# Where a streaming encoder layer splits its weights: the order of the up stage, of the weight sums, and of the last residual row

## The chip, the cores and the metric

The kernel runs on one core of one Trainium2 chip. Its time is device time in microseconds (us), the median of the runs of one kernel. A core has five engines with queues of their own, which run beside each other and wait for one another by semaphores: TensorE (PE in the profile; PEld are its weight loads), VectorE (DVE), ScalarE (ACT), GpSimd (POOL) and SyncE (SP), which here only starts DMA transfers.

## The reference, cut to what matters

One layer of an encoder over 1152 tokens (1024 of a prompt, 8 x 16 of decoding samples), all in float32:

```python
h  = rms_norm(x, g_norm_mix);  z = h @ w_in            # split into latents, keys, gates ga, gb ...
x  = x + (sigmoid(ga) * (A @ w_oa) + sigmoid(gb) * (R @ w_or)) @ w_out
u  = rms_norm(x, g_norm_ffn) @ w_ffn_up                # 1024 -> 2 x 2816, gate and value halves
c  = up[:, 0:T]*cw[0] + up[:, 1:T+1]*cw[1] + up[:, 2:T+2]*cw[2] + bias   # causal conv, width 3
x  = x + (silu(c_gate) * c_val) @ w_ffn_down
```

`A` is latent attention, `R` retention; both, and the states that are returned, are outside the change.

## The kernel before

**Precision.** Each float32 factor is split into two parts: ACT casts the high part (`whi`, `xt`, `act` ..., line 228), DVE subtracts it from the source (line 229, `wlo` and its like). A product is then three matmuls, high by high, high by low and low by high. So each weight piece that is loaded costs a cast on ACT and a subtraction on DVE before PE can use it.

**Stages around the change.** (1) The gate stage makes tiles of the gate projection; the kv stage follows later. (2) The mix stage runs three layers of eight output tiles each, `w_or`, `w_oa` and `w_out`, through `layer` (line 1243); a tile is 72 matmuls into three PSUM tiles of 384 columns, and its result is evicted by DVE (lines 1275, 1282 and, in w_out, 1294). w_out's eviction adds the residual row from `x`, and its rows go in the order 0, 4, 1, 5, 2, 6, 3, 7. (3) The up stage has 22 `Pair`s, each one gate and one value tile of 128 channels over all tokens. (4) The down stage makes 24 tiles of 66 matmuls, of which the first two are computed together.

**The pair.** The up projection of a pair is done with seven products (`products`, line 1353; n = 0 to 6) of 24 matmuls of 128 x 288 instead of eight, by Winograd's scheme: the rows are combined into seven blocks (b11, t2, b21, t3, t1, t4, b22, each in four parts over k; line 1324 and 1327 are two of the subtractions), and the weights into sums. The products accumulate in three banks: p (n = 0, 2), q (n = 1, 3, 5) and r (n = 4, 6). After some of the products `then(n, ..)` reads a bank that the next product in it goes on adding to: `read_u2` after n = 1 and `read_u3` after n = 3 (both line 1404), c11 after n = 2 (L1420), c21 and c12 at the end. Around these reads DVE and ACT do the rest of the work for the pair before: the three conv taps of value (`cv`) and gate (`cg`, taps at L1451 and L1455), Silu (L1538), the product of both (L1459, L1462), a store of the result to `s_act`, and for the pair after, the splits of its four weight pieces w[0] to w[3] (`prep(i)`; w[3] is 512 wide, the others 1024).

**Weight sums.** Three of the four pieces of a pair come from sums of weight quarters. POOL makes them (`sums`, L344 to L347) from loads of `w_up` (`prg`, `prv`, `pr`) and stores them in DRAM (`s_w`): eleven full sets in the gate stage, then the others in halves, one half after each tile of the mix stage (`presum_half`). The raw buffers of the halves are those of w[3] and its high part (tags w3, h3).

**Row blocks.** Blocks that have a place in memory during w_out are split there; the others go to DRAM (`s_t`, `s_b`) and come back as `z` (two buffers; `reload`), each with its two splits.

**What sets the order.** A scheduler orders the instructions by its own estimate, except inside `in_order(engines)`, which keeps the named engines' instructions as they are written. FOUR is PE, ACT, DVE and POOL. Before, a pair is in FOUR order, but for pair 0, where PE alone is fixed; the down stage's two first tiles are not in a fixed order. DMA queues on SP and POOL run in order.

## Time and profile before

| | us |
|---|---|
| median of 3 runs (least, most) | 2517.89 (2517.13, 2523.43) |
| profiled execution | 2519.17 |
| its span, first to last instruction | 2517.2 |
| PE, DVE, ACT, POOL busy | 2405.0, 1415.6, 938.6, 453.8 |
| mean granted clock | 0.98 |
| w_out ends, pair 0 begins | 1675.78 |
| pair 1 begins | 1716.92 |
| sixth product of pair 1, of pair 21 | 1733.31, 2224.81 |

A timeline row gives start, duration, engine, line, operation, output and inputs with their shapes, how many instructions are grouped, and in brackets the idle time before and what ended it. A row of waits gives the engine and line that waited, what for, the total, the number of times and the longest. In a chain (start, duration, what) each piece was released by the one before.

### The profile page before, as it was taken

The numbers are of one execution on the slowest core, as the hardware profiler recorded it, in microseconds if no ns is written. First come the engines' busy times: TensorE is split into PE (matmuls) and PEld (weight loads), VectorE is DVE, ScalarE is ACT, GpSimd is POOL, SyncE is SP. The second block draws the span as 40 slices with busy tenths as digits, with TensorE's granted clock in tenths as the row PEclk, the third lists the DMA queues.
The fourth block names the chain that finished last, engine by engine and source line by source line (L and its number), as shares of the span: only waits on it lengthen the run. The fifth ranks groups of instructions, "written<-read, shape, count | busy, mean of one in ns | idle before, by whom it ended". The sixth has DMA issues, their size and how long they took to land.

```text
span 2517.2 us, 38532 instructions
## 1 busy us (share of the span) xinstructions
PE 2405.0 (96%) x14888; PEld 2290.5 (91%) x14888; DVE 1415.6 (56%) x2857; ACT 938.6 (37%) x2210; POOL 453.8 (18%) x734
## 2 busy tenths in 40 slices
PE   8999999999999999999999989979999999999999
PEld 8999998898999978888999989968999999989999
DVE  6233456546259766446884235367777777775442
ACT  5121332333246555664663112243333333243331
POOL 4701001001013212331111432321000000111100
PEclk9999999999999999998999999989999999999999
DMA  7932220111125676228766555562232323367752
GB/s 266 372 127 106 94 69 23 61 63 41 64 89 177 207 241 208 95 80 220 197 170 199 190 182 176 179 213 93 92 104 91 108 94 105 103 199 240 228 165 90
DMA packets 176935, 366.29 MB, mean 146 GB/s; under 512 B 15344, under 2 KB 93296, under 8 KB 175088
## 3 DMA queue, kind: packets, MB, share of 16 engines
q1 hardware_dynamic: 82528, 213.00, 25.9%
q0 software_dynamic: 35968, 88.52, 11.4%
q10 hardware_dynamic: 58256, 62.30, 7.3%
q8 instruction: 117, 1.92, 0.3%
q14 instruction: 66, 0.54, 0.1%
HBM read 252.65 MB, written 111.13 MB: 145 GB/s over the span
## 4 chain that ended last, share of the span: by engine, by line
PE 71%; DMA 9%; DVE 9%; POOL 4%; issue 3%; ACT 3%; SPq 1%; ACTq 0%; POOLq 0%; DVEq 0%
PE mm L188 43%; PE mm L1365 16%; DMA pr<-w_up 4%; PE sm L188 4%; PE sc L188 3%; DVE wlo L229 2%; PE apo L188 2%; ACT whi L228 1%; PE apt L1126 1%; DVE cv L1459 1%; POOL psum L347 1%; POOL psum L345 1%; POOL psum L344 1%; DVE rl L229 1%; POOL psum L346 1%
## 5 line engine op out<-in xcount | busy, mean ns | idle before, releaser
L229 DVE TENSOR_TENSOR wlo<-wraw,whi 128x1024 fp32r<-128x1024 f32 (+3 forms) x223 | 260.8, 1176 | 301.2 <-ACT whi L228 300.1
L228 ACT CAST whi<-wraw 128x1024 fp32r<-128x1024 f32 (+3 forms) x223 | 217.8, 992 | 388.7 <-PE mm L188 319.6
L1365 PE MATMUL mm<-xt,whi 128*128 128x288 f32 x1408 | 291.0, 301 | 43.3 <-DVE u L1404 34.2
L1365 PEld LDWEIGHTS mm<-xt,whi 128*128 128x128 f32 x1408 | 230.8, 192 | 48.8 <-DVE u L1404 39.1
L188 PE MATMUL mm<-whi,xh 128*128 128x256 f32 (+2 forms) x720 | 228.2, 333 | 0.7 <-DVE gsig L398 0.7
L188 PE MATMUL mm<-whi,xl 128*128 128x256 f32 (+2 forms) x720 | 225.3, 329 | 0.0
L188 PE MATMUL mm<-wlo,xh 128*128 128x256 f32 (+2 forms) x720 | 224.8, 329 | 0.3 <-DVE wlo L229 0.3
L1365 PE MATMUL mm<-xb,whi 128*128 128x288 f32 x1056 | 212.2, 295 | 0.0
L1365 PE MATMUL mm<-xt,wlo 128*128 128x288 f32 x704 | 211.1, 300 | 0.0
L1365 PEld LDWEIGHTS mm<-xb,whi 128*128 128x128 f32 x1056 | 170.3, 189 | 0.3
L188 PE MATMUL mm<-rh,whi 128*128 128x384 f32 x576 | 136.8, 344 | 25.7 <-DVE mg L1294 9.1
L1365 PE MATMUL mm<-xb,wlo 128*128 128x288 f32 x528 | 156.0, 295 | 0.0
L188 PEld LDWEIGHTS mm<-whi,xl 128*128 128x128 f32 x720 | 132.5, 190 | 12.1
L188 PEld LDWEIGHTS mm<-whi,xh 128*128 128x128 f32 x720 | 132.6, 190 | 10.6 <-issue 0.7
L188 PE MATMUL mm<-act,whi 128*128 128x384 f32 x528 | 136.4, 337 | 5.8 <-ACT act L228 3.4
L188 PEld LDWEIGHTS mm<-wlo,xh 128*128 128x128 f32 x720 | 132.6, 190 | 9.8 <-DVE wlo L229 0.5
L188 PE MATMUL mm<-rl,whi 128*128 128x384 f32 x576 | 134.8, 341 | 3.6 <-DVE rl L229 3.6
L188 PE MATMUL mm<-act,dwhi 128*128 128x384 f32 x528 | 135.4, 335 | 0.0
L1365 PEld LDWEIGHTS mm<-xt,wlo 128*128 128x128 f32 x704 | 135.4, 192 | 0.0
L188 PE MATMUL mm<-rh,wlo 128*128 128x384 f32 x576 | 133.8, 340 | 0.0
L188 PEld LDWEIGHTS mm<-rh,whi 128*128 128x128 f32 x576 | 105.7, 193 | 28.5 <-ACT whi L228 9.3
L188 PE MATMUL mm<-xh,whi 128*128 128x384 f32 x528 | 123.8, 340 | 3.9 <-ACT whi L228 3.1
(492 smaller groups left out, 5679.3 us busy)
## 6 DMA issues: line engine op xcount, KB each, us to landing
wraw<-w_dn SPq DMA_DIRECT2D x48, 512.0 KB, 3.6
s_q<-uqT ACTq DMA_DIRECT2D x36, 384.0 KB, 3.1
aq<-s_q POOLq DMA_DIRECT2D x8, 1536.0 KB, 9.9
ar<-s_act POOLq DMA_DIRECT2D x21, 576.0 KB, 6.1
s_w<-psum POOLq DMA_DIRECT2D x11, 1024.0 KB, 9.6
pr<-w_up SPq DMA_DIRECT2D x44, 256.0 KB, 4.7
s_w<-psum POOLq DMA_DIRECT2D x22, 512.0 KB, 4.5
wraw<-w_up SPq DMA_DIRECT2D x22, 512.0 KB, 3.8
```

Source lines behind the costliest of these rows:

```text
L188: E.matmul(out, l, r, start=start, stop=stop)
L228: A.copy(hi, src)
L229: return V.tensor_tensor(out=lo, in0=src, in1=hi.bitcast(F32), op=ALU.subtract)
L344: G.tensor_tensor(out=s[:, 1], in0=rg[:, 0], in1=rv[:, 0], op=ALU.add)
L345: G.tensor_tensor(out=s[:, 2], in0=rv[:, 0], in1=rv[:, 1], op=ALU.add)
L346: G.tensor_tensor(out=s[:, 0], in0=s[:, 2], in1=rg[:, 0], op=ALU.add)
L347: G.tensor_tensor(out=s[:, 3], in0=s[:, 0], in1=rg[:, 1], op=ALU.add)
L1126: E.transpose(pt[:, j * 256 + e * P:j * 256 + (e + 1) * P], pm[e][:, jj * P:(jj + 1) * P], ident)
L1365: E.matmul(banks[bank][c], l[:, ks], x, start=bool(first) and k + e == 0, stop=k + e == 5, skip_group_check=not first)
L1459: V.tensor_tensor(out=cv[:, :SEQ], in0=cg[:, :SEQ], in1=cv[:, :SEQ], op=ALU.mult)
```

## The change

Up stage: within a pair the taps come first, the split of w[3] moves from the end of the pair before to n = 1 of its own pair, and the product moves ahead of `prep(0)`; the order is fixed for pair 0 too. DVE in a steady pair, from the 512 wide `wlo` (w[3]'s) or the first conv tap on (`cv`, `cg`: the taps at L1455, now L1526; `ug<-mm,ivx`: the c11 read; `cv<-cg,cv`: the product). Before:

```order
L229 TENSOR_TENSOR wlo<-wraw,whi 128x512
L1455 SCALAR_TENSOR_TENSOR cv<-uv,c_gcol,cv 128x1168
L1404 TENSOR_TENSOR u_18263<-r_18231,mm 128x288 x2
L1455 SCALAR_TENSOR_TENSOR cv<-uv,c_gcol,cv 128x1168
L1455 SCALAR_TENSOR_TENSOR cg<-ug,c_gcol,cg 128x1168 x2
L1420 TENSOR_TENSOR ug<-mm,ivx 128x288 x2
L229 TENSOR_TENSOR wlo<-wraw,whi 128x1024
L1459 TENSOR_TENSOR cv<-cg,cv 128x1024
L1462 TENSOR_TENSOR cg<-cg,cv 128x128
L1404 TENSOR_TENSOR u_18329<-mm,r_18231 128x288 x2
L229 TENSOR_TENSOR wlo<-wraw,whi 128x1024
```

Now:

```order
L1526 SCALAR_TENSOR_TENSOR cv<-uv,c_gcol,cv 128x1168 x2
L1526 SCALAR_TENSOR_TENSOR cg<-ug,c_gcol,cg 128x1168
L1475 TENSOR_TENSOR u_18252<-r_18218,mm 128x288 x2
L1526 SCALAR_TENSOR_TENSOR cg<-ug,c_gcol,cg 128x1168
L229 TENSOR_TENSOR wlo<-wraw,whi 128x512
L1491 TENSOR_TENSOR ug<-mm,ivx 128x288 x2
L1530 TENSOR_TENSOR cv<-cg,cv 128x1024
L1533 TENSOR_TENSOR cg<-cg,cv 128x128
L229 TENSOR_TENSOR wlo<-wraw,whi 128x1024
L1475 TENSOR_TENSOR u_18320<-mm,r_18218 128x288 x2
L229 TENSOR_TENSOR wlo<-wraw,whi 128x1024
```

The 512 wide `wlo` went from the head of the taps to behind them, and the product (L1459, now L1530) from behind a 1024 wide `wlo` to ahead of it; the second L1404 (now L1475) is `read_u3`.

Weight sums: loads and sums are separate, and the sums of a load come one tile later. Twelve full sets are made in the gate and kv stages instead of eleven, and twenty halves in the mix stage instead of 22. DVE in the middle of w_out (`mg` is the evicted tile, `acc` the sum of squares for the norm). Before:

```order
L229 TENSOR_TENSOR xt_17148<-t_17145,xt_17148 128x576
L1303 TENSOR_TENSOR acc<-acc,mg 128x1152
L229 TENSOR_TENSOR wlo<-wraw,whi 128x512
L1294 TENSOR_TENSOR mg<-mm,mg 128x384 x3
L229 TENSOR_TENSOR wlo<-wraw,whi 128x1024
L1320 TENSOR_TENSOR t_17371<-y 128x576
```

Now:

```order
L229 TENSOR_TENSOR xt_17145<-t_17142,xt_17145 128x576
L1320 TENSOR_TENSOR acc<-acc,mg 128x1152
L1312 TENSOR_TENSOR mg<-mm,mg 128x384 x3
L229 TENSOR_TENSOR wlo<-wraw,whi 128x1024
L1349 TENSOR_TENSOR t_17364<-y 128x576
```

Pair 0's w[3] split (`wlo` 128x512) is no longer ahead of the eviction at L1294 (now L1312).

Last row: w_out's row 7, its blocks and the reloads of the blocks are in one fixed order on ACT and DVE, with three reloads put behind the first product of pair 0 and three behind the second; two subtractions went from POOL to DVE, and the norm's steps are spread over pair 0. DVE from the first reloads (`z`) on. Before:

```order
L229 TENSOR_TENSOR xt_17568<-z,xt_17568 128x576
L229 TENSOR_TENSOR xt_17573<-z,xt_17573 128x576
L1303 TENSOR_TENSOR acc<-acc,mg 128x1152
L229 TENSOR_TENSOR xt_17578<-z,xt_17578 128x576
L229 TENSOR_TENSOR xt_17583<-z,xt_17583 128x576
L229 TENSOR_TENSOR xt_17640<-t_17626,xt_17640 128x576
L229 TENSOR_TENSOR xt_17588<-z,xt_17588 128x576
L1294 TENSOR_TENSOR mg<-mm,mg 128x384 x2
L229 TENSOR_TENSOR xt_17593<-z,xt_17593 128x576
L1294 TENSOR_TENSOR mg<-mm,mg 128x384
L229 TENSOR_TENSOR wlo<-wraw,whi 128x1024
L1321 TENSOR_TENSOR t_17627<-y,t_17626 128x576
```

Now:

```order
L229 TENSOR_TENSOR xt_17563<-z,xt_17563 128x576
L229 TENSOR_TENSOR xt_17568<-z,xt_17568 128x576
L1320 TENSOR_TENSOR acc<-acc,mg 128x1152
L229 TENSOR_TENSOR xt_17573<-z,xt_17573 128x576
L229 TENSOR_TENSOR xt_17578<-z,xt_17578 128x576
L229 TENSOR_TENSOR wlo<-wraw,whi 128x1024 x2
L1375 TENSOR_TENSOR t_17559<-y 128x576
L229 TENSOR_TENSOR xt_17599<-t_17559,xt_17599 128x576
L1312 TENSOR_TENSOR mg<-mm,mg 128x384 x3
L1378 TENSOR_TENSOR t_17560<-y,t_17559 128x576
L229 TENSOR_TENSOR xt_17613<-t_17560,xt_17613 128x576
L229 TENSOR_TENSOR xb_17616<-y,xb_17616 128x576
```

Two weight splits and `t1` with its split stand ahead of row 7's eviction (L1312), which stood behind five reloads, `acc` and one split before, with no weight split ahead of it.

Down start: the groups of activations and the weight pieces come in another order, and PE computes the first two tiles strictly by k.

The diff, cut to its core:

```diff
+def sum_load(j, p, bufs):
+    rg, rv = (p.tile([P, 2, 512], F32, name=n, bufs=bufs) for n in ("prg", "prv"))
+    with in_order(ET.SP):
+        S.dma_start(rg, quarters(d["w_up"][j]))
+        S.dma_start(rv, quarters(d["w_up"][NJ + j]))
+    return j, rg, rv
+
+def sum_store(j, rg, rv, p, bufs):
+    s = p.tile([P, 4, 512], F32, name="psum", bufs=bufs)
+    sums(s, rg, rv)
+    G.dma_start(s_w[j], s)
...
-            j = f - 2
-            rg, rv = (wk.tile([P, 2, 512], F32, name=n, bufs=2) for n in ("prg", "prv"))
-            with in_order(ET.SP):
-                S.dma_start(rg, quarters(d["w_up"][j]))
-                S.dma_start(rv, quarters(d["w_up"][NJ + j]))
-            s = wk.tile([P, 4, 512], F32, name="psum", bufs=2)
-            sums(s, rg, rv)
-            G.dma_start(s_w[j], s)
+            if f > 2:
+                pend.append(sum_load(f - 3, wk, 2))
+            if f > 3:
+                sum_store(*pend.pop(0), wk, 2)
+        sum_store(*pend.pop(0), wk, 2)
...
+            if t in (2, 5):
+                pend.append(sum_load(10 + t // 5, wk, 1))
+            elif pend:
+                sum_store(*pend.pop(), wk, 1)
...
-halves = [(j, h) for j in range(11, NJ) for h in range(2)]
+halves = [(j, h) for j in range(12, NJ) for h in range(2)]
 
 def presum_half():
-    if not halves:
-        return
-    j, h = halves.pop(0)
-    hs = slice(h * 256, (h + 1) * 256)
-    rg, rv = (fwt.tile([P, 2, 256], F32, name="pr", tag=t) for t in ("w3", "h3"))
-    with in_order(ET.SP):
-        S.dma_start(rg, quarters(d["w_up"][j])[:, :, hs])
-        S.dma_start(rv, quarters(d["w_up"][NJ + j])[:, :, hs])
-    s = wk.tile([P, 4, 256], F32, name="psum")
-    sums(s, rg, rv)
-    G.dma_start(s_w[j][:, :, hs], s)
-
-def layer(mm, w, order, fill, out, then=None):
+    if pend:
+        j, hs, rg, rv = pend.pop()
+        s = slot("psum", "e9", dt=F32)[:, :D].rearrange("p (a c) -> p a c", a=4)
+        sums(s, rg, rv)
+        G.dma_start(s_w[j][:, :, hs], s)
+    if halves:
+        j, h = halves.pop(0)
+        hs = slice(h * 256, (h + 1) * 256)
+        rg, rv = (fwt.tile([P, 2, 256], F32, name="pr", tag=t) for t in ("w3", "h3"))
+        with in_order(ET.SP):
+            S.dma_start(rg, quarters(d["w_up"][j])[:, :, hs])
+            S.dma_start(rv, quarters(d["w_up"][NJ + j])[:, :, hs])
+        pend.append((j, hs, rg, rv))
+
+def layer(mm, w, order, fill, out):
     rows, first = new_rows(mm, w, order[0], order[1], fill)
     for i, f in enumerate(order):
         ps = fm_tile(mm, bslot(d[w][f]), rows) if i > 1 else first[i]
+        out(f, ps)
         presum_half()
-        if then and i == 7:
-            then()
-        out(f, ps)
...
-    if f < 4:
-        block("b11", f, y[:, :HT])
-    else:
-        combine(f - 4)
+    return g, y
+
+def squares(g, f):
     if f:
         A.activation(g, g, AF.Square)
         V.tensor_tensor(out=acc, in0=acc, in1=g, op=ALU.add)
     else:
         A.activation(acc, g, AF.Square)
 
+ha, hb = slice(0, HT), slice(HT, T)
+late_work = []
+
...
+def reload(blocks):
+    for b, k in blocks:
         z = wk.tile([P, HT], F32, name="z", bufs=2)
         S.dma_start(z, s_t[b, k])
         block(b, k, z)
+
+def last_row(ps):
+
+    y1 = ys[3]
+    t1 = wk.tile([P, HT], F32, name="t1")
+    t2 = wk.tile([P, HT], F32, name="t2")
+    with in_order(ET.Activation, ET.DVE):
+        reload(late[:4])
+        raw = up_raw(0)
+        w = [wtile(raw[i], D, i) for i in range(2)]
+        V.tensor_tensor(out=t1, in0=y1[:, ha], in1=y1[:, hb], op=ALU.subtract)
+        block("t1", 3, t1)
+        g, y2 = res_row(7, ps)
+        V.tensor_tensor(out=t2, in0=y2[:, hb], in1=t1, op=ALU.add)
+        block("t2", 3, t2)
+        block("b21", 3, y2[:, ha])
+        V.tensor_tensor(out=y1[:, hb], in0=y1[:, hb], in1=y2[:, hb], op=ALU.subtract)
+        block("t3", 3, y1[:, hb])
+        w.append(wtile(raw[2], D, 2))
+
+    def fourth():
+        V.tensor_tensor(out=y2[:, ha], in0=y2[:, ha], in1=t2, op=ALU.subtract)
+        block("t4", 3, y2[:, ha])
+        reload(late[4:7])
+
+    def fifth():
+        block("b22", 3, y2[:, hb])
+        squares(g, 7)
+        reload(late[7:10])
+
+    late_work.extend((raw, w, fourth, fifth))
 
 order = list(range(8))
 raw_row = lambda src: (lambda t: (S.dma_start(t, src), t)[1])(wk.tile([P, T], F32, name="y", bufs=2))
 layer(mm, "w_or", order, lambda k, hi, lo: split(hi, lo, raw_row(s_ret[k])), ret_out)
 layer(mm, "w_oa", order, lambda k, hi, lo: split(hi, lo, raw_row(s_att[k])), att_out)
-layer(mm, "w_out", [0, 4, 1, 5, 2, 6, 3, 7], lambda k, hi, lo: split(hi, lo, xf[k]), res_out, reload)
+layer(mm, "w_out", [0, 4, 1, 5, 2, 6, 3, 7], lambda k, hi, lo: split(hi, lo, xf[k]), res_out)
 
 
...
+def norm_a():
     V.tensor_scalar(out=ss, in0=col_sums(sm, acc), scalar1=1.0 / D, scalar2=EPS, op0=ALU.mult, op1=ALU.add)
     rpow(i2, ss)
-    yield 1
-    iv = wk.tile([P, NU - 2], F32, name="cg")[:, :T]
-    yield from to_rows(sm, iv, i2, wk.tile([P, NU - 2], F32, name="cv")[:, :CH])
+
+def norm_b():
+    dg = wk.tile([P, NU - 2], F32, name="cv")
+    for t in range(NT):
+        V.tensor_scalar(out=dg[:, t * P:(t + 1) * P], in0=ident, scalar1=i2[:, t:t + 1], scalar2=None, op0=ALU.mult)
     V.memset(ivx, 1.0)
-    V.tensor_copy(ivx[:, 2:2 + SEQ], iv[:, :SEQ])
-    V.tensor_copy(samples(ivx)[:, :, 2:], by_seq(iv[:, SEQ:]))
+    return dg
+
+def norm_c(dg):
+    for c in range(NCH):
+        ps = sm.tile([P, 512], F32, name="sm")
+        E.matmul(ps[:, :CH], ones, dg[:, c * CH:(c + 1) * CH], start=True, stop=True)
+        n = min(CH, SEQ - c * CH)
+        A.copy(ivx[:, 2 + c * CH:2 + c * CH + n], ps[:, :n])
+    V.tensor_copy(samples(ivx)[:, :, 2:], by_seq(ps[:, n:CH]))
 
 A1, A2 = slice(2, 2 + HT), slice(2 + HT, NU)
...
             if prev:
                 prev.keep(g, prev.ug)
                 prev.tap(v, prev.uv, prev.cv, 1)
+                prev.tap(v, prev.uv, prev.cv, 0)
+                prev.tap(g, prev.ug, prev.cg, 1)
+            else:
+                fourth()
         elif n == 1:
             me.read_u2(ps)
             if prev:
-                prev.tap(v, prev.uv, prev.cv, 0)
-                prev.tap(g, prev.ug, prev.cg, 1)
                 prev.tap(g, prev.ug, prev.cg, 0)
+            else:
+                fifth()
+            w[3] = wtile(raw_w[3], 512, 3)
+            if prev:
                 A.activation(prev.cg, prev.cg, AF.Silu)
             if last:
                 me.ra = [act_raw(0, i) for i in range(3)]
                 me.rw = [down_raw(0, 0), down_raw(1, 0)]
         elif n == 2:
+            if not j:
+                open_up()
             me.read_c11(ps)
...
+                prev.product()
             if last:
                 wa.extend(down_w(me.rw[0], 0, set_a))
             else:
                 prep(0)
-            if prev:
-                prev.product()
         elif n == 3:
             me.read_u3(ps)
+            if not j:
+                norm_a()
             if last:
                 me.rw += [down_raw(0, 1), down_raw(1, 1)]
                 wb.extend(down_w(me.rw[1], 0, set_b))
-                acts.extend(act_split(me.ra[0], act_tiles(AT[0])))
+                group(0)
                 me.ra.append(act_raw(0, 3))
             else:
                 prep(1)
...
             me.past(NJ + j, me.uv)
             if j:
                 me.scale(me.uv, A2)
+            else:
+                me.dg = norm_b()
             if last:
-                acts.extend(act_split(me.ra[1], act_tiles(AT[1])))
+                group(1)
                 me.ra.append(act_raw(0, 4))
         elif n == 5:
             me.read_c21(ps)
             if j:
                 me.scale(me.uv, A1)
-                me.keep(NJ + j, me.uv)
-                me.cv = me.tap2(NJ + j, me.uv, "cv")
-            if not last:
+            else:
+                norm_c(me.dg)
+                me.scale(me.uv, slice(2, NU))
+            me.keep(NJ + j, me.uv)
+            if last:
+                me.rw.append(down_raw(0, 2))
+                group(2)
+                me.ra.append(act_raw(0, 5))
+            else:
                 prep(2)
+            me.cv = me.tap2(NJ + j, me.uv, "cv")
         else:
             me.read_c12(ps)
             me.past(j, me.ug)
-            if j:
-                me.scale(me.ug, A2)
-                me.cg = me.tap2(j, me.ug, "cg")
-            if not last:
-                prep(3)
-        if j == 0 and n >= 4:
-            if n == 4:
-                stream.now = 0
-                stream.start(nrm)
-            stream.tick()
-
-    products(w, then)
-    if j == 0:
-        stream.drain()
-        for f, u, n in ((NJ, me.uv, "cv"), (0, me.ug, "cg")):
-            me.scale(u, slice(2, NU))
-            if f:
-                me.keep(f, u)
-            setattr(me, n, me.tap2(f, u, n))
-    now.close()
-    w = nw
+            me.scale(me.ug, A2 if j else slice(2, NU))
+            me.cg = me.tap2(j, me.ug, "cg")
+
+    with in_order(*FOUR):
+        products(w, then)
+    w, raw_w = nw, raw_n
...
         wa += down_w(rw[2], 1, set_a)
+        wb += down_w(rw[3], 1, set_b)
         rw.append(down_raw(1, 2))
-        wb += down_w(rw[3], 1, set_b)
         group(3)
         ra.append(act_raw(0, 6))
         prev.tap(v, prev.uv, prev.cv, 1)
         prev.tap(v, prev.uv, prev.cv, 0)
         group(4)
         group(5)
+        prev.tap(j, prev.ug, prev.cg, 1)
+        prev.tap(j, prev.ug, prev.cg, 0)
+        A.activation(prev.cg, prev.cg, AF.Silu)
         wa += down_w(rw[4], 2, set_a)
         wb += down_w(rw[5], 2, set_b)
-        prev.tap(j, prev.ug, prev.cg, 1)
-        prev.tap(j, prev.ug, prev.cg, 0)
         group(6)
-        A.activation(prev.cg, prev.cg, AF.Silu)
         prev.product()
         acts += act_split(prev.cv[:, None, :CH], act_tiles(AT[7]))
+        ps = [bank(), bank()]
+        for k in range(NJ):
+            for q, ww in zip(ps, (wa, wb)):
+                mm3(q, ww[k], acts[k], k == 0, k == NJ - 1)
+        load_w(2)
+        load_w(3)
```

More of the change, by code (lines that the diff above doesn't have):

```diff
@@ L1254, in _body @@
         fz = ExitStack()
+        pre = big.enter_context(pool("upre"))
         wk = fz.enter_context(pool("mwork"))
@@ L1265, in block, with up_raw @@
             X[b, k] = (t[:, 0], t[:, 1])
+        def up_raw(j):
+            return [wraw(0, d["w_up"][j]), wraw(1, s_w[j][:, 0:2]), wraw(2, s_w[j][:, 2], d["w_up"][NJ + j][:, 512:]), wraw(3, s_w[j][:, 3])]
         xf = [None] * 8
@@ L1305, in res_out @@
                 A.activation(acc, g, AF.Square)
+        ha, hb = slice(0, HT), slice(HT, T)
+        late_work = []
+        def res_out(f, ps):
+            if f == 7:
+                return last_row(ps)
+            g, y = res_row(f, ps)
+            if f < 4:
+                block("b11", f, y[:, ha])
+            else:
+                combine(f - 4)
+            squares(g, f)
         def combine(k):
             y1, y2 = ys[k], ys[k + 4]
-            a, b = slice(0, HT), slice(HT, T)
             def done(name, src):
-                if (name, k) in early or k == 3:
+                if (name, k) in early:
                     block(name, k, src)
@@ L1319, in combine @@
             t2 = wk.tile([P, HT], F32, name="t2")
[L1320 to L1321 removed]
+            V.tensor_tensor(out=t1, in0=y1[:, ha], in1=y1[:, hb], op=ALU.subtract)
+            V.tensor_tensor(out=t2, in0=y2[:, hb], in1=t1, op=ALU.add)
             done("t2", t2)
[L1323 to L1325 removed]
+            done("b21", y2[:, ha])
+            G.tensor_tensor(out=y1[:, hb], in0=y1[:, hb], in1=y2[:, hb], op=ALU.subtract)
+            done("t3", y1[:, hb])
             done("t1", t1)
[L1327 to L1332 removed]
+            G.tensor_tensor(out=y2[:, ha], in0=y2[:, ha], in1=t2, op=ALU.subtract)
+            done("t4", y2[:, ha])
+            done("b22", y2[:, hb])
+        def reload(blocks):
+            for b, k in blocks:
                 z = wk.tile([P, HT], F32, name="z", bufs=2)
@@ L1406, in read_p @@
             def read_p(self, ps):
[L1407 removed]
+                self.r1 = pre.tile([P, HT], F32, name="r1")
                 for c in range(2):
@@ L1507, in _body @@
         AT = [tuple(DS[i] for i in t) for t in AT]
-        raw_w = up_raw(0)
-        w = [wtile(r, r.shape[1], i) for i, r in enumerate(raw_w)]
-        raw_w = up_raw(1)
-        nrm = norm()
+        raw_w, w, fourth, fifth = late_work
+        w.append(None)
+        raw_n = up_raw(1)
         prev = None
@@ L1517, in _body, with group @@
             nw = [None] * 4
-            now = ExitStack()
-            now.enter_context(in_order(*FOUR) if j else in_order(ET.PE))
             def prep(i):
-                r = raw_w[i]
-                nw[i] = wtile(r, r.shape[1], i)
+                nw[i] = wtile(raw_n[i], D, i)
+            def group(g):
+                acts.extend(act_split(me.ra[g], act_tiles(AT[g])))
             def then(n, ps):
@@ L1605, in _body, with load_w @@
             j, v = NJ - 1, NF - 1
+            def load_w(s):
+                if s < len(steps):
+                    ws[s] = [x for i in range(3) for x in down_w(down_raw(steps[s][1], i), i, (set_a, set_b)[s % 2])]
+            steps = [(c, f) for c in range(NCH) for f in range(8)]
+            ws = {}
+            bank = lambda: mm.tile([P, 512], F32, name="mm")[:, :CH]
             with in_order(*FOUR):
```

51 lines of the change are left out of this document (15 added, 36 removed).

## The prediction

> **What bounds the kernel now.** I read the busy shares on the page, then TensorE's (PE's) waits, then a table of windows, then timelines around the longest waits.
>
> ```profile
> span 2517.2 us, 38532 instructions
> PE 2405.0 (96%) x14888; PEld 2290.5 (91%) x14888; DVE 1415.6 (56%) x2857; ACT 938.6 (37%) x2210; POOL 453.8 (18%) x734
> ```
>
> PE is busy for 96% of the span: only its 112 us of idle time, and time at a lower clock, can be won. Its waits (total, times, longest) say where:
>
> ```profile
> PE mm L1365 <- DVE u L1404: 34.2, 21, 1.9
> PE mm L188 <- DVE mg L1294: 9.1, 1, 9.1
> PE mm L188 <- DVE xf L1275: 8.6, 1, 8.6
> PE mm L1365 <- ACT xt L228: 7.1, 1, 7.1
> PE mm L188 <- DVE mg L1282: 5.9, 4, 3.1
> PE sm L333 <- DVE diag L330: 4.6, 1, 4.6
> ```
>
> The first row is one wait in each of 21 pairs of the up stage. In the windows below (stretch, length, busy time of the engines, granted clock third from the end) the first has no wait, two are single pairs, one is twenty pairs; then come the last residual row's end with pair 0, the stretch after the w_out wait, the start of the down stage, and the rest of it.
>
> ```profile
> 1736.59:1742.95 6.36, 6.36 (x50) 6.36 (x49) 3.80 (x8) 2.30 (x2) 0.47 (x4) 1.00 0.19 60
> 1733.31:1757.58 24.27, 22.52 (x168) 22.29 (x169) 18.18 (x28) 7.84 (x9) 2.29 (x8) 1.00 0.32 99
> 1806.15:1831.89 25.74, 24.04 (x168) 23.81 (x168) 18.18 (x28) 7.84 (x9) 2.29 (x8) 0.93 0.31 95
> 1733.31:2224.81 491.50, 457.15 (x3363) 452.22 (x3363) 363.74 (x541) 158.85 (x182) 46.73 (x161) 0.99 0.32 103
> 1675.78:1716.92 41.14, 29.78 (x195) 27.79 (x195) 27.32 (x46) 16.77 (x27) 6.18 (x7) 0.88 0.42 126
> 1647.71:1653.84 6.13, 6.13 (x19) 5.84 (x20) 3.75 (x6) 3.82 (x6) 0.00 (x0) 0.50 0.81 281
> 2224.81:2264.96 40.15, 35.02 (x196) 33.42 (x197) 32.12 (x36) 19.82 (x20) 7.42 (x16) 0.96 0.72 238
> 2264.96:2517.00 252.04, 248.76 (x1435) 248.44 (x1434) 100.92 (x102) 74.00 (x76) 21.88 (x37) 1.00 0.58 181
> ```
>
> The first window is two products of 24 matmuls (n=6 of one pair, n=0 of the next): 6.36 / 48 = 0.1325 us each, a product 3.18, a pair's 168 matmuls 22.26. A pair takes 24.27, of which 24.27 - 22.52 = 1.75 is the wait. Some take 25.74 at clock 0.93, 1.47 more. Twenty pairs took 491.5 against 20 x 24.27 = 485.4, so four were of that kind. The last row shows clock 1.00 through 252 us without a gap: a denser up stage should not lose clock.
>
> **The steady pair.** VectorE (DVE) and ScalarE (ACT) before the sixth product (n=5), which PE starts at 1757.58:
>
> ```profile
> 1745.35 0.69 DVE L229 TENSOR_TENSOR wlo<-wraw,whi 128x512 fp32r<-128x512 f32 x1 [1.99 <-ACT whi L228]
> ...
> 1748.04 1.43 DVE L1455 SCALAR_TENSOR_TENSOR cv<-uv,c_gcol,cv 128x1168 f32<-128x1168 f32 x1
> 1749.39 2.90 DVE L1455 SCALAR_TENSOR_TENSOR cg<-ug,c_gcol,cg 128x1168 f32<-128x1168 f32 x2
> 1752.42 0.82 DVE L1420 TENSOR_TENSOR ug<-mm,ivx 128x288 f32<-128x288 f32 x2
> 1754.47 1.23 DVE L229 TENSOR_TENSOR wlo<-wraw,whi 128x1024 fp32r<-128x1024 f32 x1 [1.23 <-ACT whi L228]
> 1755.61 1.22 DVE L1459 TENSOR_TENSOR cv<-cg,cv 128x1024 f32<-128x1024 f32 x1
> ...
> 1757.08 0.81 DVE L1404 TENSOR_TENSOR u<-mm,r 128x288 f32<-128x288 f32 x2
> ...
> 1752.32 1.18 ACT L1538 ACTIVATE cg<-cg 128x1168 f32<-128x1168 f32 x1 [6.41 <-DVE cg L1455]
> ```
>
> The last read (L1404, of n=3) frees the bank that n=5 goes on adding to. By the product length n=1 of this pair ends at 1742.95 + 3.18 = 1746.1, n=2 at 1749.3, n=3 at 1752.5, n=4 at 1755.7. So the read's input was there 4.6 us early, but DVE works its queue in order and two waits stand ahead in it: 1.99 for w[3]'s cast at the chain's head, 1.23 for prep(0)'s cast, which ACT starts only behind the Silu. The change takes both out: the taps run first; w[3]'s split (0.69) stands behind them and the second product's read; the product goes ahead of prep(0), so that cast runs beside it. Counting on from 1745.35 - 1.99 = 1743.4, where DVE stood free: three taps of about 1.4 reach 1747.5; the read (0.8, input at 1746.1) 1748.2; the fourth tap 1749.6; w[3]'s low part 1750.2; the c11 read 1751.0; the product, whose Silu ended at 1750.8, 1752.5 with its short second half; prep(0) 1753.7; the read 1754.4. PE asks at 1755.7: 1.3 us to spare, and about 2.4 once the pair before is on time too, when the taps start a microsecond sooner within the pair. The other edges have more: c11's read is needed only by n=4, w[3] by n=6, ten microseconds behind its split. DVE works 18.2 of 22.3 us, so the bound passes to PE. Price: 20 x (24.27 - 22.26) + 4 x 1.47 = **46.1 won**, and 0.5 (0 to 0.5) in pair 1.
>
> **Sums and w_out.** The long wait in w_out:
>
> ```profile
> 1632.45 1.32 SPq L1296 DMA_DIRECT2D s_x<-mg  x1
> ...
> 1640.04 1.74 DVE L1303 TENSOR_TENSOR acc<-acc,mg 128x1152 f32<-128x1152 f32 x1 [4.51 <-ACT mg L1302]
> ...
> 1646.41 0.69 DVE L229 TENSOR_TENSOR wlo<-wraw,whi 128x512 fp32r<-128x512 f32 x1 [4.64 <-ACT whi L228]
> ...
> 1647.71 1.53 PE L188 MATMUL mm<-rh,whi 128*128 128x384 f32 x3 [9.05 <-DVE mg L1294]
> ```
>
> The eviction (L1294) of the fifth w_out tile stands on DVE behind pair 0's w[3] split, whose load waits for the last sums. SP's store of the row before, which the squares wait for, stands behind the sums' loads. The change takes w[3] out of that place and ends the sums a tile earlier. Neither is then in the way: **9.05 won**, and the half clock after it (window 1647.71, 18 matmuls, elsewhere 248.76 / 1435 = 0.173 each: 6.13 - 3.12) **3.0**; together 12.1 from above; from below 4.6, if the squares still hold the eviction up as long as the split did. I take 12.1, since both causes move.
>
> The Trainium skill, "TensorE: Matmul & The Clock Gate", section "Part 1: The HAM clock gate (the "warmup" mystery)", says the clock halves after about 3.4 us of idling and returns after about 3.4 us of sustained work. By it the 3.0 would be 1.7, and a 1.75 us wait would cost no clock; the rows above show 6.1 us at 0.50 and pairs at 0.93, and the measurement decides.
>
> Elsewhere in the mix stage sums move with their loads, so each load still follows the sums before it, and the gate rows (mg) stand behind as many sums on POOL as before. I leave those waits, 8.6 and 5.9, where they are: 0 (0 to 17 with the clock). In the gate stage POOL did the first sums ahead of the norm's power, which PE's 4.55 waited for:
>
> ```profile
> 33.92 1.83 POOL L344 TENSOR_TENSOR psum<-prg,prv 128x512 f32<-128x512 f32 x1 [32.02 <-DMA prv<-w_up]
> ...
> 39.70 0.17 DVE L436 TENSOR_SCALAR ss<-sm 128x9 f32<-128x9 f32 x1 [0.27 <-PE sm L339]
> ...
> 41.49 1.84 POOL L284 TENSOR_TENSOR inv<-ss,negh 128x9 f32<-128x9 f32 x1
> 43.30 1.25 POOL L344 TENSOR_TENSOR psum<-prg,prv 128x512 f32<-128x512 f32 x1
> ...
> 47.45 1.65 PE L333 MATMUL sm<-diag,ones 128*128 128x384 f32 x2 [4.55 <-DVE diag L330]
> ```
>
> A tile later for the sums puts the power first, at 39.9 instead of 41.5: **2 won** (0 to 4.5). The eleventh and twelfth full sets go to the kv stage (so the mix stage has 20 half sets, not 22): each is two loads on SP, four adds of about 1.3, 5.1 in all, and a store on POOL's queue, beside matmuls that run ahead of their evictions. If the norm work behind them on POOL is late by a whole set, it is 5.1 twice: **1 lost** (0 to 10).
>
> **Last row and pair 0.** The 41.14 before hold 22.3 of work, these waits, and clock 0.88:
>
> ```profile
> 1687.42 0.61 PE L1365 MATMUL mm<-xt,whi 128*128 128x288 f32 x1 [7.12 <-ACT xt L228]
> ...
> 1690.07 0.61 PE L1365 MATMUL mm<-xt,whi 128*128 128x288 f32 x1 [2.04 <-DVE xt L229]
> ...
> 1676.38 4.08 DMA z<-s_t
> ...
> 1680.48 0.68 ACT xt L228
> ...
> 1681.19 0.76 DVE xt L229
> ```
>
> A reload (z) costs 4.08 + 0.68 + 0.76 = 5.5 with its two splits, and two buffers take turns. Now everything is in a fixed order. On DVE row 7's eviction comes behind four reloads, two weight splits (1.2 each) and t1 with its split (two of 0.8); counted from the last w_out matmul it runs at 4.5 to 5.9, t2 and its two splits end at 8.7, and n=1, through with its seven earlier blocks at 5.7, waits 3.0. The next three reloads stand ahead of u2, and the third must wait for a buffer: u2 ends near 21.3, n=2 at 15.6, so n=3 waits 5.7. The last three stand ahead of u3 with b22 and row 7's squares and leave n=5 waiting 3.4. Two subtractions come over from POOL, 0.8 each on DVE and within these counts. The norm, with its nine diagonal scalings and no copy through iv, adds about 2, the clock 5. 22.3 + 3.0 + 5.7 + 3.4 + 2 + 5 = 41.4; I take **2 lost** against 41.1, for what a fixed order adds where a transfer is late (6 won to 5 lost; if no transfer is hidden, rival B).
>
> **Down start.** 40.15 before, 32.0 at full pitch (of 196 matmuls 48 at 0.1325, the others at 0.173). The first two down tiles now follow k strictly. On DVE the split of a group of activations stands ahead of the third weight pieces, and its load waits for the buffer of the group before:
>
> ```profile
> 2232.35 4.13 DMA ar<-s_act
> ...
> 2248.96 7.33 DMA wraw<-w_dn
> ```
>
> Counted from that load's issue, 4.1 to land and some 5 for the splits on ACT and DVE ahead of the pieces and their own, PE gets them 6 to 7 us after it asks. Before, it ran other groups meanwhile. With 3.0 of clock, as in w_out, that is 9 to 10 lost where before loses 8.1: **2 lost** (3 won to 5 lost). The other edits (r1 and u2 in a pool of their own, the order of stores) move nothing that is waited for: 0.
>
> **Sum** from the profiled execution, 2519.17 (span 2517.2 and 1.97 around it; the median of the runs is 1.3 below it): 2519.2 - 46.1 - 0.5 - 12.1 - 2 + 1 + 2 + 2 = **2463.5**, say 2463.
>
> **Rivals.** A: the steady wait only shrinks. DVE still has 18.2 us in a fixed order, and a cast that is late by 2 us (w[3]'s, behind the second product) brings half of it back: 20 x 1.0 + 3 of clock = 23 less won, 2486. Against it: 1.3 to 2.4 us of room.
> B: pair 0's reloads hide nothing. Three in series are 16.5; ahead of u2 and of u3, with one product of 3.2 meanwhile, that is two waits of 13.3 where I count 5.7 and 3.4: 17.5 more, 2481. For it: two buffers, and the queue order.
> C: "one tile behind" also frees the gate rows of the mix stage, 8.6 + 5.9 and 2.5 of clock: 17 less, 2446. Against it: as many sums ahead of each mg load.
> D, the slower side: the split of w[3] inside its own pair waits for its load. The buffer comes free only with the split, SP queues the reload there, and behind the split on DVE stand c11, the product, prep(0) and u3. If that load is late by more than the room of 1.3 to 2.4, n=5 waits x in every pair, and the time is 2463.5 + 20x: no change at x = 2.8, slower by more than the measurement's bound from 3.2, 2533 at 3.5. Against it: the reload is queued a pair length, 22 us, ahead, and loads here take 4 to 7.
>
> **Chances.** Forecast 0.64, B 0.09, A 0.08, C 0.07, D 0.12 (0.05 of it no change, 0.07 slower). About 0.3%, 7.6 us, is what a measurement of this kernel tells from no change: faster 0.88, same 0.05, slower 0.07. The forecast's own bounds, 2452 to 2475, widened to C and to A leave about 2 in 10 out: 2446 to 2488.
>
> **What would show it.** PE's row for the read of u gone or under 5 us, a steady pair at 22.3 to 22.5, clock 1.00 in it; no wait over 2 us in w_out; a first gate wait of about 3; pair 0 still 40 or so from the last w_out matmul to pair 1; waits for weight pieces after the last pair. A pair still above 23 makes the prediction wrong, and the last row of waits says whether through A or D.

## The result and the profile after

The changed kernel takes 2455.91 us (median of four runs, 2453.34 to 2458.73), the kernel before 2517.51 (four runs, 2512.12 to 2523.43). The ratio is 0.9755, 95% interval 0.9729 to 0.9781: 62 us, 2.4%, faster. The prediction on record was 2463 (2446 to 2488) for a profiled execution of 2519.17; the profiled execution after took 2458.73, with a span of 2456.9. So 7 us of the gain were not foreseen at the median, 4.3 in the profiled execution.

What PE waits for now, in the changed kernel (engine and line, what for, total, times, longest). The lines have moved: 1365 is now 1422, 1404 is 1475, 1275 is 1293, 1282 is 1300, 1294 is 1312.

```profile
PE mm L188 <- DVE xf L1293: 8.9, 1, 8.9
PE sm L188 <- ACT th L228: 6.6, 2, 6.1
PE mm L188 <- ACT whi L228: 5.5, 3, 3.4
PE mm L1422 <- DVE u L1475: 5.2, 1, 5.2
...
PE mm L188 <- DVE mg L1300: 3.3, 2, 2.6
...
PE sm L333 <- DVE diag L330: 2.9, 1, 2.9
```

The row that was first, 34.2 us in 21 waits for the read of u, is one wait of 5.2, and that one lies in pair 0. The 9.1 of w_out is gone altogether. The 8.9 of the mix stage stands as it was (8.6 before).

Windows of the changed kernel (stretch, length, busy time of PE, PEld, DVE, ACT, POOL, granted clock third from the end): a steady pair, the twenty pairs, and the stretch from w_out's end to pair 1.

```profile
1724.52:1746.78 22.26, 22.26 (x170) 22.26 (x169) 18.36 (x27) 8.27 (x9) 3.44 (x8) 1.00 0.35 110
1721.34:2166.60 445.26, 445.26 (x3363) 445.26 (x3362) 368.40 (x541) 168.50 (x183) 69.38 (x161) 1.00 0.35 114
...
1661.72:1705.44 43.72, 32.91 (x193) 30.61 (x193) 30.57 (x52) 19.53 (x31) 3.78 (x4) 0.84 0.41 130
```

A pair takes 22.26 with PE busy in all of it, at clock 1.00. From n=5 of pair 1 to the start of n=5 of pair 21, at 2166.54, it is 445.20, which is 20 x 22.26 (the window above ends 0.06 later). DVE in such a pair, from the first tap to the read that PE needs:

```profile
1729.22 2.90 DVE L1526 SCALAR_TENSOR_TENSOR cv<-uv,c_gcol,cv 128x1168 f32<-128x1168 f32 x2
...
1736.05 0.69 DVE L229 TENSOR_TENSOR wlo<-wraw,whi 128x512 fp32r<-128x512 f32 x1
...
1737.82 1.22 DVE L1530 TENSOR_TENSOR cv<-cg,cv 128x1024 f32<-128x1024 f32 x1
...
1740.41 0.81 DVE L1475 TENSOR_TENSOR u<-mm,r 128x288 f32<-128x288 f32 x2
```

n=0 of this pair starts at 1727.70 (1724.52 and one product of 3.18), so the read ends at 1741.2, 13.5 us into the pair, and PE asks for n=5 at 1727.70 + 15.90 = 1743.6: 2.4 us to spare.

By stage, from the timelines of both profiled executions (the ends are a w_or wait at 1340, w_out's end, n=5 of pair 1, n=5 of pair 21, the span's end):

| stretch | before | after | measured | predicted |
|---|---|---|---|---|
| gate, kv, attention | 1340.1 | 1340.5 | +0.3 | -1 |
| mix stage to w_out's end | 335.7 | 321.3 | -14.4 | -12.1 |
| last row, pair 0, to n=5 of pair 1 | 57.5 | 59.6 | +2.1 | +1.5 |
| twenty pairs | 491.5 | 445.2 | -46.3 | -46.1 |
| rest | 292.4 | 290.4 | -2.0 | +2 |
| span | 2517.2 | 2456.9 | -60.3 | -55.7 |

### The profile page after: what moved, and what is told of

The parts are those of the page before. It is cut to its first block, busy times and chain, and to the rows that moved or that the text cites. A ratio compares the mean times of both kernels' runs of the same rounds, so it can differ in the third digit from the quotient of the medians.

```text
span 2456.9 us, 38559 instructions
## 1 busy us (share of the span) xinstructions
PE 2392.1 (97%) x14888; PEld 2284.6 (93%) x14888; DVE 1420.9 (58%) x2858; ACT 946.4 (39%) x2210; POOL 476.5 (19%) x727
## 4 chain that ended last, share of the span: by engine, by line
PE 78%; DMA 6%; issue 5%; DVE 5%; POOL 4%; ACT 2%; SPq 0%; ACTq 0%; POOLq 0%; DVEq 0%
PE mm L188 48%; PE mm L1422 19%; PE sm L188 4%; DMA pr<-w_up 3%; PE sc L188 3%; PE apo L188 2%; PE apt L1140 1%; POOL psum L344 1%; DVE wlo L229 1%; POOL psum L346 1%; DMA mg<-s_gate 1%; DMA s_x<-mg 1%; POOL psum L345 1%; DMA s<-s_ret 1%; POOL psum L347 1%
## 5 line engine op out<-in xcount | busy, mean ns | idle before, releaser
L1422 PE MATMUL mm<-xt,whi 128*128 128x288 f32 x1408 | 284.7, 297 | 6.8 <-DVE u L1475 5.2
L188 PEld LDWEIGHTS mm<-whi,xl 128*128 128x128 f32 x720 | 132.5, 190 | 12.1
L188 PE MATMUL mm<-xl,whi 128*128 128x384 f32 x528 | 122.1, 337 | 0.0
```

The lines of the kernel that those rows point to most:

```text
L188: E.matmul(out, l, r, start=start, stop=stop)
L1422: E.matmul(banks[bank][c], l[:, ks], x, start=bool(first) and k + e == 0, stop=k + e == 5, skip_group_check=not first)
```

## The experiments

Each kernel is the changed one with the edit shown. The times of single runs stand beside 2455.91 for the changed kernel; where a few microseconds count, the trace of the stage is what is read.

**Which edit frees the steady pair.** The pair's order has four edits: w[3]'s split in its own pair, the product ahead of `prep(0)`, `prep(2)` ahead of the value's last tap on ACT (`tap2`), and all but one tap ahead of the second product's read. Two accounts: the place of w[3]'s split is what won, or only the sum of what stands ahead of the read counts, so that one edit can stand in for another. First w[3]'s split alone goes back:

```diff
 # n == 1
-w[3] = wtile(raw_w[3], 512, 3)
+if not prev: w[3] = wtile(raw_w[3], 512, 3)
 # n == 6, at the end
+if not last: nw[3] = wtile(raw_n[3], 512, 3)
```

> Theory (queue order on DVE and ACT; each of the four edits of the pair is in reserve for the others): only w[3]'s split goes back to the end of the pair before. Counted on with the durations of the rows, the read of n=3 then ends 14.5 us into the pair instead of 13.3, and PE asks at 15.9: no wait, pairs of 22.3, twenty of them in 445, the time that of the changed kernel within 5 us. Rival (the place of w[3]'s split is what won the 46 us): a wait of 1 to 1.8 before n=5 in every pair, pairs of 23.3 to 24.3, 20 to 45 us more.

Measured: 2461.53 us, and a single wait of 0.2 in twenty pairs. Then only w[3]'s split stays. The diff gives what is written behind each product (v and g are taps of value and gate, u2 and c11 the reads):

```diff
-n=0: v1 v0 g1;  n=1: u2 g0 w3;  n=2: c11 product prep(0);  n=5: c21 prep(2) tap2
+n=0: v1;  n=1: u2 v0 g1 g0 w3;  n=2: c11 prep(0) product;  n=5: c21 tap2 prep(2)
```

> Only w[3]'s split stays in its new place; the product goes behind prep(0) again, prep(2) behind the last tap's scaling on ACT, and two of the taps behind the second read. Theory (queue order): the read of n=3 ends at 16.4, 0.5 late; with the 0.3 by which this count is short for the kernel before, a wait of 0.4 to 0.8 before n=5, pairs of 22.7 to 23.1, 10 to 17 us more than the changed kernel. Rival (w[3]'s place is what won): no wait, 22.3.

Measured: 2477.8 us, twenty waits of about 0.5, 10.0 in all, pairs of 461.12 / 20 = 23.06. Then only the taps stay (the first diff, and of the second n=2 and n=5):

> Only the taps stay ahead of the second read; w[3]'s split, the product and prep(2) are back. Theory (queue order): the wait moves, since the taps now hold up the second read: about 0.9 before n=3 and 0.5 before n=5, pairs of 23.7 to 24.1, 28 to 36 us more than the changed kernel. Rival (one wait with one cause): 1.4 to 1.8 before n=5 alone, or none.

Measured: 2504.48 us, and two waits a pair. Two rows of PE's timeline in one pair of it, n=3 and n=5:

```profile
1763.14 0.53 PE L1422 MATMUL mm<-xt,whi 128*128 128x288 f32 x2 [1.15 <-DVE u L1475]
...
1770.10 0.53 PE L1422 MATMUL mm<-xt,whi 128*128 128x288 f32 x2 [0.33 <-DVE u L1475]
```

And with all four undone:

> All four edits of the pair's order undone, the rest of the change kept. Theory (these four are the whole gain of the steady pair): one wait of 1.4 to 1.8 before n=5, pairs of 23.7 to 24.3, the twenty pairs in 474 to 491, 30 to 46 us more than the changed kernel. Rival (the rest of the change, such as weight pieces loaded from the pair before on, won part of it): pairs under 23.3.

Measured: 2515.74 us. The windows of the four, in this order, each from n=1 of a pair to n=1 of pair 21; the first two hold twenty pairs, the others nineteen:

```profile
1708.30:2153.95 445.65, 445.48 (x3362) 445.24 (x3361) 363.67 (x540) 163.42 (x183) 46.37 (x161) 1.00 0.34 110
```

```profile
1706.77:2167.89 461.12, 450.70 (x3363) 445.88 (x3361) 364.86 (x544) 157.93 (x181) 68.54 (x160) 1.00 0.33 106
```

```profile
1731.20:2192.32 461.12, 433.05 (x3194) 424.23 (x3193) 345.44 (x514) 148.87 (x171) 43.15 (x152) 1.00 0.31 101
```

```profile
1735.47:2203.06 467.59, 434.18 (x3194) 429.70 (x3193) 345.40 (x514) 148.88 (x171) 43.18 (x152) 0.99 0.31 100
```

That is 22.28, 23.06, 24.27 and 24.61 us a pair. What follows: the four edits together are the whole gain of the steady pair, since without them it is as before (491.5 / 20 = 24.58), and the rest of the change adds nothing to it. The place of w[3]'s split, which the change is named for, is enough for most of the gain but not needed for any: with it alone back nothing is lost, and with it alone kept a pair loses 0.80 of 2.35, so two thirds are won. The product's place, `prep(2)`'s and the taps' were not undone one at a time, so that each of them can be spared in the same way is not shown.

The taps' place without the rest wins nothing in the common pair, which takes 24.27 as before: the wait is split in two, and the first part stands before n=3. What lies between 24.27 and 24.61 is slower pairs of 25.8 (the clock is 0.99 over that window), which do not come behind waits of 1.15 and 0.33 (1.00). A pair is also longer than its waits tell: PE's busy time in it is 22.26 without a wait, 450.70 / 20 = 22.54 with one and 433.05 / 19 = 22.79 with two, so each wait costs some 0.27 beyond itself.

Three of the four times lie further above the changed kernel than was expected: 21.9 where 10 to 17 was, 48.6 where 28 to 36 was, 59.8 where 30 to 46 was; the first, 5.6, is just outside its 5. For the last, the twenty pairs from n=5 of pair 1 take 48.2 more, pair 1 up to its n=5 3.4 and the stretch behind n=5 of pair 21 5.9; the expectations counted the twenty pairs alone.

**The sums in the mix stage and w_out.** The sums end one tile later again:

```diff
 # layer
-out(f, ps)
-presum_half()
+if w != "w_or" or i > 0: presum_half()
+out(f, ps)
```

> Only the half sums of the mix stage go back by one tile, so that the last is made beside the sixth w_out tile as before; pair 0's w[3] split stays out of w_out. Theory (two things held the w_out eviction, w[3]'s split and the squares of the row before, whose store stands behind the sums' loads on SP): the squares alone hold it, a wait of 2 to 5 us before the w_out tile behind the fifth eviction (before, the squares ended at 1641.8 and the eviction began at 1647.0, 9.05 - 5.2 = 3.8). Rival (w[3]'s split alone made the 9.05): no wait over 1 us in w_out.

Measured: 2459.0 us. The waits of PE in its mix stage:

```profile
PE mm L188 <- DVE mg L1301: 5.2, 3, 3.7
...
PE mm L188 <- DVE mg L1313: 2.3, 1, 2.3
```

2.3 us for the eviction in w_out (here L1313): the squares hold it for a part, as expected. In the kernel before, by its own rows, w[3]'s split held it for another 5.2, from the squares' end at 1641.8 to 1647.0. In the changed kernel both are out of the way. That w[3]'s split in its old place makes the rest was not tried by itself. The 8.9 of the first layer is not in this kernel, which makes no half sum beside the first w_or tile, but the waits at L1301 are longer than the changed kernel's 3.3. In all its mix stage takes 315.4 (1344.97 to 1660.36) against 321.3, and 318.5 to 322.0 in the variants that leave this stage as it is: what the changed kernel does with the sums lost more elsewhere in this stage than it won in w_out.

**The gate stage's sums** ahead of the norm's power again:

```diff
-if f > 2: pend.append(sum_load(f - 3, wk, 2))
-if f > 3: sum_store(*pend.pop(0), wk, 2)
+if f < 12: sum_store(*sum_load(f - 2, wk, 2), wk, 2)
```

> Only the gate stage's loads and sums go back by one tile, ahead of the norm's power on POOL. Theory (POOL's order made the first gate wait): the first wait is 4.5 again instead of 2.9, and PE is 1.5 to 3 us later in what follows. Rival (the wait comes from the norm's own chain): 2.5 to 3.2, nothing later.

Measured: 2461.33 us, and the first gate wait:

```profile
47.83 1.65 PE L333 MATMUL sm<-diag,ones 128*128 128x384 f32 x2 [4.83 <-DVE diag L330]
```

So POOL's order made 1.9 of that wait. PE is also later in what follows, by 3.2 at the end of the kv stage (642.06 against 638.86) and 3.6 at the w_or wait near 1340 (1344.09 against 1340.46). Why the kernel before shows no such loss at 1340 is told below.

**The gate rows of the mix stage.** In the forecast the 8.6 and 5.9 were left standing, because the gate rows' loads (`mg`) stand behind as many sums on POOL as before. The text of the changed kernel puts each load ahead of the sums of the tile before; the scheduler did not keep that. In the changed kernel's w_or, the load for two tiles (L1290) stands behind sums that wait 6.81 for their own load, and the eviction waits for it:

```profile
1430.03 0.73 POOL L344 TENSOR_TENSOR psum<-pr 128x256 f32<-128x256 f32 x1 [6.81 <-DMA pr<-w_up]
...
1434.04 1.18 POOL L1290 DMA_DIRECT2D mg<-s_gate  x2
...
1439.50 1.49 DVE L1293 TENSOR_TENSOR xf<-mm,mg 128x384 f32<-128x384 f32 x3 [13.46 <-DMA mg<-s_gate]
```

Here POOL is held to the written order:

```diff
-out(f, ps)
-presum_half()
+with in_order(ET.Pool) if w != "w_out" else ExitStack():
+    out(f, ps)
+    presum_half()
```

> In the changed kernel POOL's instructions of the w_or and w_oa tiles are kept as they are written, each tile's gate rows (mg) ahead of the sums of the tile before. Theory (the gate rows stand behind sums that wait for their loads): the waits for DVE at L1293 (8.9) and L1300 (2.6 and 0.7) go, to under 1.5 in all, and the slow clock behind the first, 10 to 15 us less. Rival (the gate rows' own transfer is late, or the sums, now later, hold up w_out): over 5 us of wait stay in the mix stage, gain under 5.

Measured: 2437.74 us, 18 less than the changed kernel. What PE waits for from 1340 to 1645:

```profile
PE mm L1423 <- ACT whi L228: 1.6, 1, 1.6
PE mm L1423 <- DVE wlo L229: 1.3, 1, 1.3
PE mm L188 <- DVE mg L1301: 0.6, 1, 0.6
PE mm L188 <- DVE rl L229: 0.2, 1, 0.2
```

The 8.9 and 2.6 are gone and with them the clock behind them (in the changed kernel 0.53 from 1453.62 to 1460.20 and 0.61 from 1509 to 1516). From the w_or wait that ended at 1340 in the changed kernel to w_out's end it takes 302.4 us (1337.46 to 1639.89) instead of 321.3, 18.9 less and more than the 10 to 15 expected. This is the forecast's rival C, "one tile behind also frees the gate rows", priced at 17: it did not come with the change, but it was there to be had.

**The reloads of pair 0.** The splits of w[0] and w[1] ahead of the reloads, three reloads behind the second product's read and three behind the fourth and fifth product. These last three also come through a buffer of their own (`cg`'s) and not through z's two, here and in the next run:

```diff
-last_row: reload(late[:4]); w[0], w[1];  n=0: reload(late[4:7]);  n=1: u2, reload(late[7:10])
+last_row: w[0], w[1]; reload(late[:4]);  n=1: u2, reload(late[4:7]);  n=3: u3, norm_a, reload(late[7:9]);  n=4: norm_b, reload(late[9:10])
```

> In the changed kernel the splits of w[0] and w[1] go ahead of the first four reloads, the t4 reloads behind the second product's read, the b22 reloads behind the fourth product's. Theory (the reloads in front of u2 and of the weight splits on DVE make pair 0's waits): the 0.9 and 1.3 at the start of pair 0 and the 5.2 before n=3 go, to under 1.5 in all; from w_out's end to pair 1 it takes 32 to 37 us instead of 43.7, the whole 7 to 12 less. Rival (the reloads' transfers are the bound, wherever they stand): the wait moves to n=5 or n=6, the stretch stays over 40.

Measured: 2457.62 us; 40.56 us from w_out's end to pair 1. What PE waits for in that stretch:

```profile
PE sm L1458 <- DVE cv L1451: 4.1, 1, 4.1
PE mm L1421 <- ACT xt L228: 3.3, 1, 3.3
PE mm L1421 <- DVE u L1481: 1.6, 1, 1.6
```

The waits at the start and before n=3 are gone, and others have come: 3.3 before the last block of n=1, which row 7's eviction feeds, and 4.1 for the norm's diagonals, which had been done under the old wait. The rival's "over 40" is what came, but not for its reason: the stretch now has three other waits for work that stands in a fixed order on DVE and ACT. So two reloads instead of four ahead of row 7, and the norm's sums earlier:

```diff
-last_row: reload(late[:4]);  n=1: u2, reload(late[4:7]);  n=2: c11, prep(0);  n=3: u3, norm_a, reload(late[7:9])
+last_row: reload(late[:2]);  n=0: reload(late[2:4]);  n=1: u2, reload(late[4:6]), load of late[6];  n=2: norm_a, splits of late[6], c11;  n=3: u3, prep(0), reload(late[7:9])
```

> After the run before: two reloads instead of four ahead of row 7's eviction, the others spread over pair 0 behind the reads that PE waits for, the norm's sums behind the third product. Theory (every wait in pair 0 is work that stands ahead of what PE needs on DVE, and can be moved): no wait over 2 us from w_out's end to pair 1, the stretch 33 to 36 us instead of 43.7. Rival (ten reloads through two buffers take some 25 us wherever they stand): 38 to 42.

Measured: 2444.34 us; 37.05 us for the stretch, between the two accounts, and one wait over 2:

```profile
PE sm L339 <- DVE acc L1320: 3.7, 1, 3.7
PE mm L1425 <- ACT r L1490: 1.2, 1, 1.2
```

6.7 of the 43.7 were the order on DVE and ACT together with the place of the last three reloads; the two were not separated. The 3.7 is the squares of row 7, and it is order again: their store starts at 1654.98, and ACT squares the row at 1665.40 and DVE adds it up at 1667.21, each straight behind other splits and reads, without a wait. What of the rest is the reloads' transfers was not separated. (Its time is 11.6 below the changed kernel's median, more than the stretch gives; most of the rest lies ahead of the mix stage, where the two kernels are the same.)

**The start of the down stage.** Ahead of the third weight pieces stands a split that does not belong to the first two tiles: it is of the next column block, put there by the scheduler. Held back:

```diff
 if f == 3:
+    with issue_after(last ACT instruction of the fixed order), issue_after(last DVE instruction of it):
         nxt = [x for g in range(4) for x in act_group(c + 1, g)]
```

> In the changed kernel the splits of the next column block's first activation groups are held behind the start of the down stage. Theory (one such group stands ahead of the third weight pieces on DVE and ACT and waits for its load): the wait of 3.4 and 0.4 behind the last pair goes to under 0.7, the stretch from there on 2 to 4 less, no new wait when those groups are used eight tiles later. Rival (the weight pieces' own load is late): over 2 us of wait stay.

Measured: 2451.22 us. PE's two waits there:

```profile
2186.59 0.61 PE L188 MATMUL mm<-act,whi 128*128 128x384 f32 x2 [1.50 <-ACT whi L228]
2187.59 0.44 PE L188 MATMUL mm<-act,wlo 128*128 128x384 f32 x1 [0.38 <-DVE wlo L229]
```

1.9 in place of 3.8, and the stretch from n=5 of pair 21 to the end 287.5 instead of 290.4. The foreign split made half of the wait; the other half, which was expected to go too, stays, and its cause was not looked into further.

**Three of these together** (POOL's written order in w_or and w_oa, the second version of pair 0, the groups held):

> Three edits together: POOL's written order in w_or and w_oa, the reloads and the norm as in the run before, the next column block's groups held. Theory: their gains add, since they lie in three stages: 20 + 6 to 10 + 2 to 4 less than the changed kernel, 2422 to 2432. Rival (a gain upstream only lengthens the next wait): above 2436, the time of POOL's order alone.

Measured: 2428.79 us, median of five runs (2424.46 to 2433.53); 0.9646 of the kernel before, 95% interval 0.9626 to 0.9667, and 27 us below the changed kernel. The gains add: 19.6 in the mix stage (1338.35 to 1640.04 instead of 321.3), 5.3 from w_out's end to pair 1 (the window below, instead of 43.72), 2.9 at the end: 27.8.

```profile
1640.04:1678.48 38.44, 31.91 (x193) 29.85 (x193) 27.82 (x49) 18.52 (x30) 2.90 (x4) 0.87 0.37 121
```

## Why the prediction was right, point by point

**The steady pair** (46.1 predicted, 46.3 measured). PE bound at 168 x 0.1325, the read 2.4 early, the clock at 1.00: each as counted. What the forecast did not have is the attribution. It named two waits ahead of the read, w[3]'s cast and `prep(0)`'s, and did not mention `prep(2)`'s move; the runs show that w[3]'s split, which it put first, could have stayed where it was. Rival A, that the wait only shrinks, is near what w[3]'s place alone gives, 2478; rival D had no trace: no pair waits for w[3]'s load.

**w_out** (12.1 predicted). The 9.05 and the clock behind it went as priced, and the low end, in which the squares still hold the eviction, did not come; the run with late sums shows that end, with 2.3. The 2.3 that the mix stage gave beyond it are waits for gate rows at L1282, now L1300 (5.9 before, 3.3 after), which the forecast left at 0 with the gain as its bound.

**Gate and kv** (2 won, 1 lost predicted, 0.3 lost measured up to 1340). The first wait went from 4.55 to 2.91, 1.6 by POOL's order as argued. The kv stage cost nothing. Further on PE was even 2.7 ahead, and then nearly level. The same instruction in both, first of before, then of the changed kernel, in the gate tile made at the end of the kv stage:

```profile
641.60 0.79 PE L188 MATMUL mm<-xh,whi 128*128 128x384 f32 x3 [0.76 <-DVE gsig L398]
...
887.85 0.33 PE L188 MATMUL sm<-th 128*128 128x128 f32 x1 [3.22 <-ACT th L228]
```

```profile
638.86 0.79 PE L188 MATMUL mm<-xh,whi 128*128 128x384 f32 x3 [0.76 <-DVE gsig L410]
...
887.38 0.48 PE L188 MATMUL sm<-th 128*128 128x128 f32 x1 [6.11 <-ACT th L228]
```

2.7 us ahead at 640, 0.5 ahead at 887: the later wait is 2.9 longer. The lead is the change's: counted from where PE begins the first gate wait, it comes to the first of these rows after 598.7 us in the kernel before, 599.1 with the gate's sums back, and 595.7 to 597.0 in the changed kernel and its ten other variants. The longer wait is not: its length follows a load that is sometimes slow, whatever the kernel (last section). Compared like with like the lead is still there at 1340. Of the executions with a wait for `th` over 6, the one with the gate's sums back gets there after 1301.1 and the four others after 1297.6 to 1298.6; of those with a wait under 4, the kernel before after 1297.2 and the six others after 1291.8 to 1295.2. So the forecast's 1 won was too little, and the measured +0.3 is a gain of some 2 to 3, hidden by the slow load. (Both old orders have one execution each.)

**Last row and pair 0** (2 lost predicted, 43.7 - 41.1 = 2.6 measured; with pair 1's 0.5 won, 2.1). The mechanism was the one told, DVE's fixed order: the read of u stands behind a reload's split that waits for its transfer.

```profile
1683.11 0.76 DVE L229 TENSOR_TENSOR xt<-z,xt 128x576 fp32r<-128x576 f32 x1 [3.02 <-ACT xt L228]
1683.79 0.81 DVE L1475 TENSOR_TENSOR u<-r,mm 128x288 f32<-128x288 f32 x2
...
1684.29 0.85 PE L1422 MATMUL mm<-xt,whi 128*128 128x288 f32 x2 [5.17 <-DVE u L1475]
```

The terms: before n=3 5.7 against 5.17 measured; at n=1 3.0 against 1.2 + 0.4; before n=5 3.4 against none, since the wait before n=3 gave u3 its time. Not foreseen were 0.9 and 1.3 at n=0, where the splits of w[0] and w[1] themselves stand behind four reloads, and 1.2 before n=2. In all the waits are 10.8 against 12.1 counted, while PE is busy for 32.9 of the stretch against 22.3 + 2 + 5 = 29.3: the term of the norm and the clock (here 0.84) was 3.6 too small. The counted sum, 41.4, would have been 2.3 short; that the 2 lost came out is in part the margin taken on top of it.

**Down start** (2 lost predicted, 2 won measured). The step that failed is the size of one term: the third pieces come 3.8 late (3.40 and 0.38), not 6 to 7, and the clock behind them costs 1.6 and not 3.0 (below). The chain was the right one. The load of the foreign group starts at 2185.46, lands 4.57 later, its split, the Silu and the pieces' cast follow, as these rows of the chain show:

```profile
2185.46 4.57 DMA ar<-s_act
...
2190.11 1.15 ACT act L228
2191.26 0.98 ACT cg L1705
2192.25 0.82 ACT whi L228
...
2193.09 0.97 DVE wlo L229
```

Counted from the load's issue to PE at 2194.11 that is 8.7, near the 9 of the forecast; but PE, which first works on the first two pieces' matmuls, asked at 2189.71, 4.3 after the issue and not 2 to 3.

**The clock.** Behind the waits of 3.40 and of 5.17 in the changed kernel:

```profile
2193.11:2197.00 3.89, 3.50 (x11) 3.15 (x12) 3.89 (x4) 2.79 (x3) 1.06 (x2) 0.58 0.64 187
...
1684.29:1690.00 5.71, 5.71 (x30) 5.71 (x30) 3.67 (x5) 1.66 (x3) 0.00 (x0) 0.63 0.48 139
```

Each cost about 1.6 to 2.1 us of work on top of the wait (3.89 x 0.42, 5.71 x 0.37), less than the 3.0 that was taken from w_out for the down start. The Trainium skill, "TensorE: Matmul & The Clock Gate", section "Part 1: The HAM clock gate (the "warmup" mystery)", has half speed until about 3.4 us of sustained work, from which 1.7 is an estimate; these two waits agree with it, the 6.13 us at 0.50 behind the 9.05 of the kernel before do not.

**The whole.** The forecast is near because its largest term is right. Of the four smaller stages two came out with the other sign than forecast, the gate's by a slow load and the down stage's by the size of a term; the errors, in the order of the table, are +1.3, -2.3, +0.6, -0.2 and -4.0.

## What to carry to other kernels

When an engine works its queue in order and another waits for one instruction in it, add up everything that stands ahead of that instruction, waits included, against the time at which it is asked for: what counts is the total, and of several moves that each cut it, one alone may win nothing (the taps here) and one undone may lose nothing (w[3]'s split). Look for the next such wait in the same way: the largest gain left here, 18.9 us, was the order of loads and sums on POOL, which the program's text already had right and the schedule did not. And where a stretch holds a wait whose length varies from execution to execution, compare executions in which it fell alike: here a gain of some 2 to 3 us read as a loss of 0.3.
